# Later row sums, more products held in PSUM, and a depthwise convolution on TensorE alone

## The chip, the cores and the metric

The kernel runs on one core of a Trainium2 chip. The metric is device time in microseconds (us) of one execution.

## The reference

Two blocks follow each other on x of 256 tokens by 1024 channels, in float32. The first has two layers of four attention-like mixers and a gated MLP, the second four layers (retention, conformer convolution, short convolution, retention), each followed by a squared-ReLU MLP. Every stage begins with an RMS norm, which needs the sum of x's squares over the channels for each token. What the change touches, cut from the reference:

```python
def rms_norm(x, g):
    y = xf * lax.rsqrt(jnp.mean(xf * xf, axis=-1, keepdims=True) + RMS_EPS)
    return (y * g.astype(F32)).astype(x.dtype)

def conformer_conv_mixer(x, w_pw1, b_pw1, w_dw, b_dw, ln_g, ln_b, w_pw2, b_pw2):
    h = x @ w_pw1 + b_pw1
    a, gate = jnp.split(h, 2, axis=-1)
    h = a * jax.nn.sigmoid(gate)
    h = causal_depthwise_conv(h, w_dw) + b_dw          # 31 taps for each channel
    mean = jnp.mean(hf, axis=-1, keepdims=True)
    var = jnp.mean(jnp.square(hf - mean), axis=-1, keepdims=True)
    hf = (hf - mean) * lax.rsqrt(var + LN_EPS) * ln_g + ln_b
    h = jax.nn.silu(hf)
    return h @ w_pw2 + b_pw2
```

## The kernel before

x lies with channels on partitions: eight blocks of 128 channels by 256 tokens. A weight matrix product is made in three products of halves (high by high, high by low, low by high), each 128 rows by 128 columns of weights by 256 tokens: `fm_mm` (L294 to L296), and `fm_first` (L325 to L328) for four output blocks at once while x's halves `xh` and `xl` are still being made. `tm_mm` (L301 to L303) has tokens as output rows and 512 weight columns. Weights stream in 636 chunks on SyncE's queue; ScalarE casts the high half (L238), VectorE subtracts for the low half (L239). There are eight PSUM banks.

The norm's factor r is applied behind the first products, so these run on unnormed x. `prep` makes xh and xl of a quarter of x and has ScalarE square it; `stat` is a generator that lets some program steps pass (a step is 12 products), has VectorE add the four quarters of squares (L502, L505), and has TensorE sum them over partitions: `row_sums` (L395) in block 2, `token_sums` (L389) in block 1. `have_r` lets the main program wait, in program order, until r is set. Each stage starts some products before it asks for r and holds their results in PSUM. TensorE executes in program order, so a row sum whose squares are late holds up all products behind it. The order of the program is set by `main` and a `Weave`: at each step of the main generator, every generator in its `light` list advances by one step too.

The conformer's stage takes eight blocks through the gate (`glu`: scale by r, L1429; sigmoid, L1432; product into `cf_p`, padded by 30 tokens, L1435) and then 31 taps. Blocks 0, 1, 6 and 7 are convolved on VectorE (L1374, L1376), block 2 on ScalarE and GpSimd (L1443, L1444), blocks 3 to 5 on TensorE by 31 matmuls each with diagonal 128 by 128 matrices (L1454), which GpSimd builds earlier (L1390). Low halves go to GpSimd in that time (`lo_engine`). Sums for mean and variance come together on VectorE (L1504) and TensorE (L1521, bank `cm`); normalisation and halves `cf_h` and `cf_l` follow block by block, and the last product `cf_w_pw2_2` into the banks `acc`. In the retention, `rotary` (L1309 to L1312) turns q and k on VectorE, then TensorE makes the scores in `bk_ra`, VectorE masks them into `rt_a` (L1266), and TensorE makes the output products `bk_ry` (L1274).

Of the kernel before, what the change touches and what calls it, by code (L numbers as in the profile page):

```python
# [17 lines left out]
P = 128  # L18
# [10 lines left out]
CF_PE = (3, 4, 5)  # L29
CF_DVE = ((0, 1), (6, 7))  # L30
CF_POOL = (2,)
CF_STEP = 4
CF_LATE = 4
CF_GLU = 1
LAG_COLS = (8, 3)
LAG_ROWS = 9
WARM1 = (0, 10, 0, 0)
RET_PRE = 1
# [4 lines left out]
LAG_FINAL = 8  # L43
# [107 lines left out]
for _n, _w in (("norm_mix", 16), ("norm_ffn", 16), ("norm_final", 8), ("norm_g", 128), ("gn_g", 32),  # L151
               ("b_pw1", 16), ("w_dw", 31 * 8), ("b_dw", 8), ("ln_g", 8), ("ln_b", 8), ("b_pw2", 8),
# [39 lines left out]
class Net:  # L192
# [277 lines left out]
    def prep(self, j, gain, final=None):  # L470
# [4 lines left out]
        self.square(j)  # L475
        if j == 3:
            self.r = None
            self.weave.light.append(self.stat(final, False))

    def square(self, j):  # L480

        q = self.g("sq")
        self.sqs = [q] if j == 0 else self.sqs + [q]
        self.nc.scalar.activation(q, self.x[j], AF.Square)

    def add_squares(self, final):
# [14 lines left out]
        for j in range(1, 4):  # L501
            add(q[0], q[0], q[j], op=ALU.add)  # L502
            yield
# [5 lines left out]
    def stat(self, final, root):  # L509
# [101 lines left out]
    def ffn(self, l):  # L611
# [3 lines left out]
        def up(f):  # L615
            sp = [((f * P, P),), ((f * P + P, P),)]
            if f == 0:
                g, u = yield from self.fm_first(l, (("w_gate", sp[0]), ("w_gate", sp[1]), ("w_up", sp[0]), ("w_up", sp[1])))
                ready.append((yield from self.fm_pair("w_gate", l, [((q * P, P),) for q in (2, 3)])))
            else:  # L620
                g = ready.pop() if ready else (yield from self.fm_pair("w_gate", l, sp))
                u = yield from self.fm_pair("w_up", l, sp)
# [510 lines left out]
    def layer1(self, l):  # L1133
# [14 lines left out]
        qb = yield from self.fm_pair("w_in", l, [cols(("a_q", 0, P)), cols(("a_q", P, P))])  # L1148
        y, rb, rb2 = yield from self.have_r()
# [7 lines left out]
        nc.vector.tensor_tensor(zq, qb, rb2, op=ALU.mult)  # L1157
        t1 = yield from self.tm_group("w_in", l, cols("c_i", "c_f", "a_g", "c_v", "a_vs", "a_vw"))
# [7 lines left out]
        zbq = yield from self.fm_scaled(l, [cols(("b_q", 0, P)), cols(("b_q", P, P))], "zbq")  # L1166
# [213 lines left out]
    def diag_taps(self, pool):  # L1380

        self.dg = {}
        for c in CF_PE:
            d = self.t([P, 31, P], "cf_d%d" % c, pool=pool)
            self.dg[c] = d
        for _ in range(12):
            yield
        for c in CF_PE:
            for q in range(31):
                self.nc.gpsimd.tensor_scalar(self.dg[c][:, q, :], self.ident, self.vec("w_dw", q * 8 + c), None, op0=ALU.mult)  # L1390
                if q % 2:
                    yield
# [437 lines left out]
```

## Time and profile before

| | |
|---|---|
| three runs | 2206.72 us median, 2206.69 to 2210.83 |
| profiled execution | 2207.37 us, its span 2205.5 us |
| mean granted TensorE clock | 0.973 of full |
| TensorE busy with matmuls | 2076.8 us, 94% |
| VectorE busy | 1508.8 us, 68% |
| ScalarE busy | 1071.0 us, 49% |
| GpSimd busy | 175.8 us, 8% |

The span is the time from the first to the last recorded instruction, and 1.9 us of the execution's time lie around it. In the rows below, PE is TensorE, PEld its weight loads, DVE VectorE, ACT ScalarE and POOL GpSimd. A float32 matmul leaves two records. In brackets stands how long the engine idled before a record, and for whom.

### The profile page before, as it was taken

The page shows a single profiled execution, that of the slowest core. Times are in us where ns is not written, and L with a number is a line of the kernel's source. Part 1 is how long each engine was busy: PE and PEld are TensorE (multiplying, and loading weights), DVE is VectorE, ACT ScalarE, POOL GpSimd, SP SyncE. Part 2 cuts the span into 40 slices and gives each one's busy share as a digit, 9 for nine tenths or more (in the row PEclk, how much of TensorE's full clock was granted, in tenths as well). Part 3 has the DMA queues.
Part 4 walks back from the last instruction along what each step waited for, and adds up shares of the span by engine and source line. Part 5 has one row for each costly group of instructions (what it writes and reads, how often), then busy time and mean ns, then how long its engine had stood idle before and what let it go on. Part 6 is the DMA issues. An engine that isn't in the chain of part 4 may idle for free.

```text
span 2205.5 us, 40772 instructions
## 1 busy us (share of the span) xinstructions
PE 2076.8 (94%) x16352; PEld 2004.2 (91%) x16352; DVE 1508.8 (68%) x2944; ACT 1071.0 (49%) x2118; POOL 175.8 (8%) x196
## 2 busy tenths in 40 slices
PE   8989999999999899989998689999989999998998
PEld 7879999878999889989997589999989988998998
DVE  6776556677755776675579985558865577667555
ACT  5445445445544444554453364444454454455443
POOL 0000000000000000193007620000000000000000
PEclk9989999999999999999999899999999999999999
DMA  7225554323655533645544035554545554464552
GB/s 272 77 78 172 186 197 154 117 86 108 201 192 182 167 133 136 205 140 192 190 137 142 11 101 185 182 185 144 194 140 192 191 171 136 148 211 145 184 183 82
DMA packets 96174, 344.49 MB, mean 156 GB/s; under 512 B 12016, under 2 KB 12272, under 8 KB 95728
## 3 DMA queue, kind: packets, MB, share of 16 engines
q1 hardware_dynamic: 95840, 341.61, 46.2%
q8 instruction: 128, 2.10, 0.4%
q14 instruction: 62, 0.51, 0.1%
q10 hardware_dynamic: 144, 0.28, 0.0%
HBM read 340.79 MB, written 1.05 MB: 155 GB/s over the span
## 4 chain that ended last, share of the span: by engine, by line
PE 74%; DVE 19%; ACT 4%; issue 2%; DMA 1%; SPq 0%; ACTq 0%; DVEq 0%
PE bk_fm L294 11%; PE bk_fm L295 11%; PE bk_fm L296 11%; PE bk_acc L295 9%; PE bk_acc L296 9%; PE bk_acc L294 9%; DVE lo L239 5%; DVE cf_c L1376 4%; PE bk_tm L301 2%; PE bk_tm L302 2%; PE bk_tm L303 2%; DVE sq L502 1%; PE bk_ss L395 1%; ACT at_s L759 1%; ACT hi L238 1%
## 5 line engine op out<-in xcount | busy, mean ns | idle before, releaser
L239 DVE TENSOR_TENSOR lo<-raw,hi 128x512 fp32r<-128x512 f32 x1240 | 782.9, 688 | 149.2 <-ACT hi L238 148.9
L238 ACT CAST hi<-raw 128x512 fp32r<-128x512 f32 x1272 | 701.5, 619 | 121.5 <-issue 67.0
L294 PE MATMUL bk_fm<-xh,hi 128*128 128x256 f32 x2400 | 690.7, 288 | 0.0
L295 PE MATMUL bk_fm<-xl,hi 128*128 128x256 f32 x2400 | 681.6, 284 | 0.0
L296 PE MATMUL bk_fm<-xh,lo 128*128 128x256 f32 x2400 | 680.5, 284 | 0.0
L294 PE MATMUL bk_acc<-hh,hi 128*128 128x256 f32 x1696 | 473.4, 279 | 0.0
L295 PE MATMUL bk_acc<-hl,hi 128*128 128x256 f32 x1696 | 473.2, 279 | 0.1
L296 PE MATMUL bk_acc<-hh,lo 128*128 128x256 f32 x1696 | 473.0, 279 | 0.0
L294 PEld LDWEIGHTS bk_fm<-xh,hi 128*128 128x128 f32 x2400 | 460.0, 192 | 5.7 <-issue 4.0
L295 PEld LDWEIGHTS bk_fm<-xl,hi 128*128 128x128 f32 x2400 | 459.8, 192 | 1.2
L296 PEld LDWEIGHTS bk_fm<-xh,lo 128*128 128x128 f32 x2400 | 459.7, 192 | 0.0
L295 PEld LDWEIGHTS bk_acc<-hl,hi 128*128 128x128 f32 x1696 | 319.1, 188 | 0.5 <-DVE hl L441 0.5
L296 PEld LDWEIGHTS bk_acc<-hh,lo 128*128 128x128 f32 x1696 | 318.9, 188 | 0.0
L294 PEld LDWEIGHTS bk_acc<-hh,hi 128*128 128x128 f32 x1696 | 318.9, 188 | 0.0
L663 DVE TENSOR_TENSOR ff_t<-ff_t 128x512 f32<-128x512 f32 x64 | 44.5, 695 | 232.5 <-ACT ff_t L662 232.5
L662 ACT ACTIVATE ff_t<-bk_fm 128x512 f32<-128x512 f32 x64 | 38.3, 599 | 250.8 <-PE bk_fm L296 249.7
L440 ACT CAST hh<-ff_t 128x512 fp32r<-128x512 f32 x102 | 63.4, 622 | 124.5 <-DVE ff_t L663 58.4
L441 DVE TENSOR_TENSOR hl<-ff_t,hh 128x512 fp32r<-128x512 f32 x102 | 70.8, 694 | 71.5 <-ACT hh L440 71.5
L1390 POOL TENSOR_SCALAR cf_d<-ident,vecs 128x128 f32<-128x128 f32 x93 | 80.7, 887 | 405.1 <-DVE ff_t L1356 405.1
L325 PE MATMUL bk_fm<-xh,hi 128*128 128x256 f32 x384 | 98.3, 288 | 15.2 <-ACT xh L1673 7.9
L326 PE MATMUL bk_fm<-xh,lo 128*128 128x256 f32 x384 | 97.3, 285 | 0.1
L301 PE MATMUL bk_tm<-hi,xh 128*128 128x512 f32 (+2 forms) x224 | 89.2, 398 | 0.0
(413 smaller groups left out, 2474.4 us busy)
## 6 DMA issues: line engine op xcount, KB each, us to landing
raw<-in_w SPq DMA_DIRECT2D x634, 512.0 KB, 4.4
cw<-in_cw SPq DMA_DIRECT2D x2, 1024.0 KB, 8.4
dt<-in_c SPq DMA_DIRECT2D x2, 768.0 KB, 4.8
x<-in_x SPq DMA_DIRECT2D x4, 256.0 KB, 5.8
raw<-in_w SPq DMA_DIRECT2D x4, 256.0 KB, 5.5
out_y<-x SPq DMA_DIRECT2D x4, 256.0 KB, 2.5
c<-in_c SPq DMA_DIRECT2D x1, 977.0 KB, 10.0
rows<-in_rows SPq DMA_DIRECT2D x1, 456.0 KB, 8.5
```

The lines of the kernel that those rows point to most:

```text
L238: nc.scalar.copy(hi[:, q], raw)
L239: self.lo_engine.tensor_tensor(lo[:, q], raw, hi[:, q].bitcast(F32), op=ALU.subtract)
L294: mm(out, w[0], x[0], start=start, stop=False, skip_group_check=True)
L295: mm(out, w[0], x[1], start=False, stop=False, skip_group_check=True)
L296: mm(out, w[1], x[0], start=False, stop=stop, skip_group_check=True)
L301: mm(out, xh, w[0], start=start, stop=False)
L325: mm(b, w[0], hi, start=k == 0 and i % 2 == 0, stop=False, skip_group_check=True)
L326: mm(b, w[1], hi, start=False, stop=False, skip_group_check=True)
L440: nc.scalar.copy(hi, src)
L441: nc.vector.tensor_tensor(lo, src, hi.bitcast(F32), op=ALU.subtract)
L1376: v.scalar_tensor_tensor(out, src[:, j:j + S], w(j), out, op0=ALU.mult, op1=ALU.add)
L1390: self.nc.gpsimd.tensor_scalar(self.dg[c][:, q, :], self.ident, self.vec("w_dw", q * 8 + c), None, op0=ALU.mult)
```

## The change

Row sums: `stat` takes two numbers, the step at which the adds begin and the step at which the sum is made. In block 1 that is 2 and 9 (adds from 4 and the sum at 8 before), in block 2 6 and 17 (from 5 and at 9), at the final norm 2 and 16. Outside the final norm two of the three adds of quarters are now issued in `prep` already. So that there are products to run until r is there, `ffn` holds a pair of `w_up` blocks too, `layer1` the pair b_q, the retention a second pair (k of head 1), the short convolution two more pairs.

Conformer: all blocks are convolved on TensorE. For each block and each quarter of 32 channels, a transfer on ScalarE's queue makes a copy of 128 partitions, 32 channels by 4 shifts of one token (`cf_x`, four buffers). A matmul with 128 rows and 32 columns (`cf_dg`, built on GpSimd from a table) then does four taps of 32 channels at once. Eight of them cover 32 taps, and four such groups write the four quarters of a bank's partitions: 32 matmuls for each block, 256 in all. The gate's order, the moments and the normalisation stay, with operations of GpSimd moved to VectorE. The last product takes its first five rows for all eight outputs, then the other three output by output.

```diff
-LAG_COLS = (8, 3)
-LAG_ROWS = 9
+LAG_COLS = ((2, 9), 4)
+LAG_ROWS = (6, 17)
-RET_PRE = 1
+RET_PRE = 2
-LAG_FINAL = 8
+LAG_FINAL = (2, 16)
...
         self.square(j)
+        if not final and j > 1:
+            self.add_square(j - 1)
...
-        for _ in range((LAG_FINAL - 6) if final else LAG_ROWS - 4 if root else LAG_COLS[0] - 4):
-            yield
-        yield from self.add_squares(final)
+        add_at, sum_at = LAG_FINAL if final else LAG_ROWS if root else LAG_COLS[0]
+        yield from self.steps(add_at)
+        n = 0
+        for _ in self.add_squares(final):
+            n += 1
+            yield
+        yield from self.steps(sum_at - add_at - n)
...
+        for c in range(NK):
+            w = taps[:, 32 * c:32 * c + 32, None].to_broadcast([P, 32, 32])
+            nc.gpsimd.tensor_tensor(self.dg[:, 32 * c:32 * c + 32, :], eye, w, op=ALU.mult)
...
+            x = self.t([P, 4, CF_U], "cf_x", F32, CF_X, p2)
+            for g in range(4):
+                a = pads[c][32 * g:32 * g + 32, 0:CF_U]
+                src = bass.AP(tensor=a.tensor, offset=a.offset, ap=[a.ap[0], [1, 4], [1, CF_U]])
+                nc.scalar.dma_start(out=x[:, g, :], in_=src)
+            xs[c] = x
+
+        def conv(c):
+
+            yield from self.until(lambda: c in xs)
             b = self.bank("cf")[:, :S]
-            for q in range(31):
-                mm(b, self.dg[c][:, q, :], pads[c][:, q:q + S], start=q == 0, stop=q == 30)
-                if q % 4 == 3:
+            x = xs.pop(c)
+            for m in range(8):
+                for g in range(4):
+                    mm(b[32 * g:32 * g + 32, :], self.dg[:, 32 * c + 8 * g + m, :], x[:, g, 4 * m:4 * m + S], start=m == 0, stop=m == 7)
+                if m % 4 == 3:
                     yield
...
-        for os in ((0, 1, 2, 3), (4, 5), (6,), (7,)):
-            for k in range(NK):
-                for o in os:
-                    b, opens = self.block(acc, o)
-                    self.fm_mm(b, self.take("cf_w_pw2_2", j, k, ((o * P, P),)), hs[k], k == 0 and opens, k == NK - 1)
-                if len(os) > 1 or k % 4 == 3:
+        for k in range(CF_ROWS):
+            for o in range(NK):
+                b, opens = self.block(acc, o)
+                self.fm_mm(b, self.take("cf_w_pw2_2", j, k, ((o * P, P),)), hs[k], k == 0 and opens, False)
+                if o % 4 == 3:
                     yield
+        for o in range(NK):
+            b, _ = self.block(acc, o)
+            for k in range(CF_ROWS, NK):
+                self.fm_mm(b, self.take("cf_w_pw2_2", j, k, ((o * P, P),)), hs[k], False, k == NK - 1)
+            yield
+            f(o)
```

How this moves the instructions is shown at three places. The first is TensorE in the MLP of block 2's first layer, at the row sum (a row is line, operation, what is written and read, and the shape). Before, the sum stands in the middle of the third pair of output blocks:

```order
L294 MATMUL bk_fm_10998<-xh7_89,hi_10850 128x256
L295 MATMUL bk_fm_10998<-xl7_97,hi_10850 128x256
L296 MATMUL bk_fm_10998<-xh7_89,lo_10851 128x256
L395 MATMUL bk_ss_11033<-sq_10823,ones_100 128x256
L294 MATMUL bk_fm_10998<-xh0_82,hi_10885 128x256
L295 MATMUL bk_fm_10998<-xl0_90,hi_10885 128x256
```

Now it stands in the middle of the next pair, behind the rest of the pair above, 48 products of the second weight matrix into `bk_acc` and half of its own pair:

```order
L294 MATMUL bk_fm_11141<-xh7_89,hi_11007 128x256
L295 MATMUL bk_fm_11141<-xl7_97,hi_11007 128x256
L296 MATMUL bk_fm_11141<-xh7_89,lo_11008 128x256
L395 MATMUL bk_ss_11175<-sq_10823,ones_100 128x256
L294 MATMUL bk_fm_11141<-xh0_82,hi_11041 128x256
L295 MATMUL bk_fm_11141<-xl0_90,hi_11041 128x256
```

The sum has moved behind 96 more products of 128x256. The second place is TensorE at the end of the conformer's first projection. Before, two blocks of 31 taps follow the last projection product, then the first mean of two blocks (`bk_cm0`), the third block of taps, and the moments (`bk_cm`):

```order
L296 MATMUL bk_fm_13787<-xh7_89,lo_13671 128x256
L1454 MATMUL bk_cf_13872<-cf_p3_13253,cf_d3_10866 128x256 x31
L1454 MATMUL bk_cf_13986<-cf_p4_13255,cf_d4_10867 128x256 x31
L1491 MATMUL bk_cm0_14089<-cf_c0_13239,mean1_6191 128x256
L1491 MATMUL bk_cm0_14089<-cf_c1_13240,mean1_6191 128x256
L1454 MATMUL bk_cf_14096<-cf_p5_13257,cf_d5_10868 128x256 x31
L1521 MATMUL bk_cm_14180<-cf_sum0_14094,ones_100 128x256
L1521 MATMUL bk_cm_14180<-cf_sum1_14095,ones_100 128x256
L1521 MATMUL bk_cm_14180<-cf_c5_13244,ones_100 128x256
L1521 MATMUL bk_cm_14180<-cf_p5_13257,ones_100 128x256
L1655 MATMUL bk_warm_14185<-hi_13670 128x256 x14
```

Now two blocks of taps stand earlier, between projection pairs, and six follow the last projection product in one go, up to the moments:

```order
L296 MATMUL bk_fm_13770<-xh7_89,lo_13583 128x256
L1447 MATMUL bk_cf_13854<-cf_x_13619,cf_dg_10868 32x256 x32
L1447 MATMUL bk_cf_13889<-cf_x_13624,cf_dg_10868 32x256 x32
L1447 MATMUL bk_cf_13928<-cf_x_13732,cf_dg_10868 32x256 x32
L1447 MATMUL bk_cf_13975<-cf_x_13849,cf_dg_10868 32x256 x32
L1447 MATMUL bk_cf_14019<-cf_x_13967,cf_dg_10868 32x256 x32
L1447 MATMUL bk_cf_14058<-cf_x_14012,cf_dg_10868 32x256 x32
L1513 MATMUL bk_cm_14101<-cf_sum0_13186,ones_100 128x256
L1513 MATMUL bk_cm_14101<-cf_sum1_13187,ones_100 128x256
L1513 MATMUL bk_cm_14101<-cf_c7_13161,ones_100 128x256
L1513 MATMUL bk_cm_14101<-cf_p7_13183,ones_100 128x256
```

The VectorE work that stood between the taps and the moments has no counterpart. The third place is VectorE in the first retention, from k's rotary of head 0 to the mask of its scores. Before, only q of head 1 (`rt_q` from `tr_qc` and `tr_qs`) is turned ahead of the mask (last row):

```order
L1312 TENSOR_TENSOR rt_k_8830<-rt_u_8828,rt_w_8829 128x256
L1340 TENSOR_SCALAR rt_s_8836<-rt_s_8836 128x2
L1342 TENSOR_SCALAR rt_v_8835<-rt_v_8835,rt_s_8836 128x512 x2
L534 SCALAR_TENSOR_TENSOR x0_78<-x0_78,vecs_98,y1_8666 128x256
L1309 TENSOR_TENSOR rt_u_8843<-bk_fm_8746,tr_qc_8813 128x512
L1310 TENSOR_TENSOR rt_w_8844<-bk_fm_8746,tr_qs_8815 128x512
L1311 TENSOR_TENSOR rt_q_8845<-rt_u_8843,rt_w_8844 128x256
L1312 TENSOR_TENSOR rt_q_8845<-rt_u_8843,rt_w_8844 128x256
L239 TENSOR_TENSOR lo_8861<-raw_8654,hi_8860 128x512
L534 SCALAR_TENSOR_TENSOR x0_78<-x0_78,vecs_98,y1_8666 128x256
L1266 TENSOR_TENSOR rt_a_8873<-bk_ra_8868,dt_8495 128x384
```

Now both q and k of head 1 are turned ahead of it:

```order
L1355 TENSOR_SCALAR rt_s_8901<-rt_s_8901 128x2
L1357 TENSOR_SCALAR rt_v_8900<-rt_v_8900,rt_s_8901 128x512 x2
L1324 TENSOR_TENSOR rt_u_8907<-bk_fm_8746,tr_qc_8878 128x512
L1325 TENSOR_TENSOR rt_w_8908<-bk_fm_8746,tr_qs_8880 128x512
L1326 TENSOR_TENSOR rt_q_8909<-rt_u_8907,rt_w_8908 128x256
L1327 TENSOR_TENSOR rt_q_8909<-rt_u_8907,rt_w_8908 128x256
L1324 TENSOR_TENSOR rt_u_8914<-bk_fm_8811,tr_kc_8882 128x512
L1325 TENSOR_TENSOR rt_w_8915<-bk_fm_8811,tr_ks_8884 128x512
L1326 TENSOR_TENSOR rt_k_8916<-rt_u_8914,rt_w_8915 128x256
L1327 TENSOR_TENSOR rt_k_8916<-rt_u_8914,rt_w_8915 128x256
L239 TENSOR_TENSOR lo_8924<-raw_8694,hi_8923 128x512
L1281 TENSOR_TENSOR rt_a_8938<-bk_ra_8933,dt_8495 128x384
```

One rotary of four operations has moved ahead of the mask.

## Rows read from the trace of the kernel before

**Rows 1.** The page's parts 1 and 4: busy time by engine, and the last chain.

```profile
PE 2076.8 (94%) x16352; PEld 2004.2 (91%) x16352; DVE 1508.8 (68%) x2944; ACT 1071.0 (49%) x2118; POOL 175.8 (8%) x196
...
PE 74%; DVE 19%; ACT 4%; issue 2%; DMA 1%; SPq 0%; ACTq 0%; DVEq 0%
```

**Rows 2.** TensorE's waits: us in all, times, longest.

```profile
PE bk_ss L395 <- DVE sq L505: 31.8, 8, 6.8
PE bk_cm L1521 <- DVE cf_sum L1504: 19.4, 1, 19.4
PE bk_ss L389 <- DVE sq L505: 10.3, 4, 4.9
...
PE bk_cf L1454 <- issue: 7.7, 1, 7.7
...
PE bk_acc L295 <- DVE cf_l L1551: 3.8, 4, 1.5
```

**Rows 3.** Row sums on TensorE and VectorE's add before one, in order of time.

```profile
753.21 2.05 PE L395 MATMUL bk_ss<-sq,ones 128*128 128x256 f32 x4 [6.84 <-DVE sq L505]
...
971.61 0.51 DVE L505 TENSOR_TENSOR sq<-sq 128x256 f32<-128x256 f32 x1
...
972.17 1.22 PE L395 MATMUL bk_ss<-sq,ones 128*128 128x256 f32 x2 [6.25 <-DVE sq L505]
...
1163.61 0.70 PE L395 MATMUL bk_ss<-sq,ones 128*128 128x256 f32 x2 [1.73 <-DVE sq L505]
...
1811.54 0.70 PE L395 MATMUL bk_ss<-sq,ones 128*128 128x256 f32 x2 [1.31 <-DVE sq L505]
```

**Rows 4.** Two windows: us, busy (records) of PE, PEld, DVE, ACT, POOL, clock, DMA, GB/s.

```profile
972.83:978.06 5.23, 5.23 (x26) 5.14 (x25) 3.75 (x7) 1.59 (x4) 5.23 (x8) 0.53 0.29 100
...
983.67:989.35 5.68, 5.68 (x51) 5.68 (x49) 2.62 (x5) 1.15 (x2) 5.68 (x8) 1.00 0.89 303
```

**Rows 5.** A window of weight products alone; of the engines PE only.

```profile
1164.00:1194.00 30.00, 30.00 (x254) 1.00 0.41 141
```

**Rows 6.** First retention: a window of one rotary (DVE), and the mask.

```profile
774.27:776.35 2.08, 2.04 (x6) 1.00 0.00 0
...
777.26 0.55 DVE L1266 TENSOR_TENSOR rt_a<-bk_ra,dt 128x384 f32<-128x384 f32 x1
```

**Rows 7.** Windows of the conformer's stage, columns as in the fourth group.

```profile
1147.11:1195.66 48.55, 46.77 (x386) 46.09 (x386) 43.80 (x67) 24.85 (x47) 31.49 (x18) 1.00 0.36 122
...
1203.38:1246.14 42.76, 42.76 (x190) 36.89 (x190) 42.30 (x65) 19.87 (x41) 35.69 (x37) 0.96 0.07 25
...
1265.55:1274.31 8.76, 7.30 (x30) 6.38 (x30) 4.83 (x13) 3.76 (x8) 0.79 (x1) 0.67 0.01 2
...
1274.31:1302.20 27.89, 24.01 (x192) 22.93 (x193) 21.73 (x38) 19.29 (x39) 10.60 (x12) 1.00 0.35 114
```

**Rows 8.** L1454: a window of it alone (PE, PEld); its loads' shortest, median, longest ns.

```profile
1210.00:1240.00 30.00, 29.30 (x137) 25.51 (x136) 1.00 0.05 19
...
L1454 PEld LDWEIGHTS bk_cf<-cf_p,cf_d x186: 187/189/337, 1203.3 to 1245.6; 128*128 128x128 f32 x186
```

**Rows 9.** Tiles of 64 rows: two first records, a window of such tiles (PE).

```profile
142.87 0.39 PE L745 MATMUL bk_s<-dl_k,dl_q 64*128 64x128 f32 x2
...
142.87:144.48 1.61, 1.61 (x17) 1.00 0.01 5
```

**Rows 10.** The conformer's first gate on VectorE.

```profile
1167.72 0.69 DVE L1429 TENSOR_TENSOR ff_t<-bk_fm,rb 128x512 f32<-128x512 f32 x1
1169.27 1.12 DVE L1435 SCALAR_TENSOR_TENSOR cf_p<-ff_t,vecs 128x256 f32<-128x256 f32 x1 [0.85 <-ACT ff_t L1432]
```

**Rows 11.** The page's part 6: a transfer, KB each, us from issue to landing.

```profile
out_y<-x SPq DMA_DIRECT2D x4, 256.0 KB, 2.5
```

More of the change, by code (lines that the diff above doesn't have):

```diff
@@ L500, in add_squares @@
             self.sq2 = t
-        for j in range(1, 4):
-            add(q[0], q[0], q[j], op=ALU.add)
+        for j in range(self.added + 1, 4):
+            self.add_square(j)
             yield
@@ L1399, in conformer @@
         for c in range(NK):
[L1400 removed]
+            a = self.t([P, 32 + S], "cf_p%d" % c, F32, 1, p2)
             nc.gpsimd.memset(a[:, 0:30], 0.0)
+            nc.gpsimd.memset(a[:, 30 + S:], 0.0)
             pads.append(a)
[L1403 to L1425 removed]
+        ready, xs = [], {}
         def glu(c, b, rb2):
@@ L1504, in fold, with after, sp @@
                     e.tensor_tensor(t, a[folded[0]] if len(folded) == 2 else t, a[c], op=ALU.add)
[L1506 to L1516 removed]
+        def after(c, b):
+            nc.scalar.activation(cv[c], b, AF.Identity, bias=self.vec("b_dw", c))
+            yield
+            if c == 1:
+                b = self.bank("cm0")[:, :S]
+                for n in range(2):
+                    mm(b, self.mean1, cv[n], start=n == 0, stop=n == 1)
+                m0.append(self.t([P, S], "cf_m0", F32, 1, p2))
+                nc.scalar.activation(m0[0], b, AF.Identity, scale=NK / 2.0)
+                yield
+            for n in (0, 1) if c == 1 else (c,) if c else ():
+                moments(n, nc.vector)
+                yield
+                fold(n, nc.vector)
+        def sp(b):
+            return ("cf_w_pw1_2", ((b * P, P),))
+        light = self.weave.light
+        begun = 0
+        for c in range(NK + CF_LAG):
+            if c == 0:
+                ready.extend((yield from self.fm_first(j, [sp(0), sp(8), sp(1), sp(9)])))
+            elif 1 < c < NK:
+                ready.append((yield from self.fm_pair("cf_w_pw1_2", j, [sp(c)[1], sp(8 + c)[1]])))
+            if c > 3:
+                _, _, rb2 = yield from self.have_r()
+            if CF_LAG <= c:
+                b = yield from conv(c - CF_LAG)
+                if c - CF_LAG < NK - 1:
+                    light.append(after(c - CF_LAG, b))
+            while c > 3 and ready and begun < CF_X + max(0, c - CF_LAG + 1):
+                light.append(glu(begun, ready.pop(0), rb2))
+                begun += 1
+            if c == NK + CF_LAG - 2:
+                self.want_sqrt()
+        last = NK - 1
+        yield from self.until(lambda: len(folded) == last)
+        nc.scalar.activation(cv[last], b, AF.Identity, bias=self.vec("b_dw", last))
         moments(last, nc.vector)
```

152 lines of the change are left out of this document (43 added, 109 removed).

## The prediction

> **What bounds the kernel now.** I read the page first: TensorE is busy 94% of the span, VectorE 68%, and of the chain that ended last 74% lies on TensorE and 19% on VectorE [rows 1]. So time comes off only where TensorE idles, runs at its lower clock, or does work that goes. The waits of TensorE come next [rows 2]: 31.8 us in eight waits at the row sums (L395) and 10.3 us in four at the column sums (L389), each for the last add of x's squares on VectorE, then 19.4 us for the conformer's moments, 7.7 us before its first tap product and 3.8 us for halves of its last product. Third, one of these places in order of time [rows 3]: the add that ends the sum starts at 971.61 and the sum at 972.17, after 6.25 us of idling; three of the eight are in other kinds of stage (6.84 and 1.31 in the retentions, 1.73 in the conformer). Fourth, what a wait costs beyond itself [rows 4]: after that one, 26 records take 5.23 us at a granted clock of 0.53, the lower level, 1.2 GHz; a little later 51 take 5.68 at 1.00 (2.4 GHz). At the second rate 26 would take 2.90, so the wait costs 2.3 us more. In a long stretch 254 weight products take 30.00 us, 0.118 each [rows 5].
>
> **The sums ahead of the MLPs and the short convolution.** The three other kinds of stage set apart, five waits are left: 31.8 - 6.84 - 1.73 - 1.31 = 21.9 us. The sum moves 96 products back, 96 x 0.118 = 11.3 us; idling began at 972.17 - 6.25 = 965.9, so TensorE comes to it at 977.2. VectorE's own end hardly moves: in its queue two adds come earlier and the last two stand behind the same hidden halves as now with one low half more ahead, so 972.1 becomes about 973. The margin is some 4 us. Held pairs are products that ran anyway. What is late next is r, by 11 us; in an MLP its reader is the stage's end. With 21.9 goes the clock: four of the five waits are long, 4 x 2.3 = 9 at most. I take **-30** (-22 if the clock stays low for other reasons, -31 with all).
>
> **The column sums in block 1.** 10.3 us of waits, and clock: once the 2.3 of above for the longest (4.9), half of it for the two of about 2, together about 3.4. The sum now has 12 products more ahead, and the adds begin two steps earlier. Not all stays: the first layers' chain from r through the scaling to the convolution and rope now has one scaling more ahead of it on VectorE, so I give 5 back for waits behind it: **-8.5** (bounds 0 and -13.7).
>
> **Retention.** The sum goes behind 36 more products of 512 columns and the pair for k of head 1 is held too. Its 6.84 goes. But VectorE does a further rotary before the scores' mask (L1266 at 777.26), whose like for q fills 774.27 to 776.35, 2.1 us [rows 6], and the sum itself comes 1.7 us later than now, since TensorE gets to it only at 746.4 (where the idling before 753.21 began) + 36 x 0.236 = 754.9; 0.236 is an estimate, twice 0.118 for twice the columns. So the first output products come about 3.8 us later than now, with 48 products (5.7) more done by then: **-2** for the first retention, 0 for the second, where 1.31 is all there was. Bounds -6 and +5, the latter if the waits for the mask come twice.
>
> **The conformer.** Its stage is 48.55 + 7.7 + 42.76 + 19.4 + 8.76 + 27.89 = 155.1 us now [rows 7, 2]: products of the first projection, wait, 93 tap matmuls on TensorE, wait for VectorE's taps, moments and normalisation, last product. The taps on VectorE, GpSimd and ScalarE go, and with them the 19.4.
>
> The new tap matmuls are the unknown. There are 256 with 32 output columns and 128 rows, each two records like the 186 of now, which take 29.30 us for 137, 0.214 each [rows 8]. Four of them write the four quarters of the output's partitions. If the four share the array perfectly, 64 groups x 2 x 0.214 = 27.4 us; one after another, 512 x 0.214 = 109.6. No row has tiles that share all rows and split the columns. The nearest have 64 rows each: two of their records start within 0.03 us of each other, and 16, half of 256 columns and half of 128, take 1.61 us (the 17th in the row is a product that ends there) [rows 9], where one after another 8 x 0.214 + 8 x 0.107 = 2.57 is due and in perfect pairs 1.28. That is 1.25 of the perfect time, end of the pipe included, which a long stretch pays less often. Between 27.4 and 27.4 x 1.25 = 34 I take **31**.
>
> The Trainium skill, "TensorE: Matmul & The Clock Gate", Part 3 (Packing small matmuls), gives 2.38 times for three column tiles of 32 and 3.07 for four row tiles; by 2.38 the taps would take 109.6/2.38 = 46 us, an estimate from that page, and the time would be 15 us above mine. No run here shows it yet.
>
> New stage: 384 products of the first projection, 45.4; the sum, 0.4; the wait for the first shifted copies, 3; taps 31; a first mean of four records 0.9; the end of the moments and the normalisation 8.8 as now; the last product 192 x 0.118 = 22.7 with 0.5 of waits, since its first five rows go over all eight outputs and leave each next half eight products' time; at its end 0.5; clock after the waits 2. Together 115.2 of 155.1: **-40** (-44 with perfect tiles, +39 one after another). The 3 us is worked out so: from the sum at 1163.61 [rows 3] to the gate's first step at 1167.72 are 4.1 us, that step starts a chain that ends at 1169.27 + 1.12 [rows 10], 2.7 us, and a transfer of 256 KB lands after 2.5 us [rows 11]; these 9.3 stand against 72 products, 8.5 us. That leaves 0.8, and the copies of four blocks may queue behind each other, so 0 to 8.
>
> At nothing I put GpSimd's eight builds of the new stationaries (the 93 builds of now go, and GpSimd is 8% busy), the 32 small transfers on ScalarE's queue, and the low halves that return from GpSimd to VectorE, which loses its taps. If the builds were late the first tap matmul would wait for them.
>
> **Sum.** -30 - 8.5 - 2 - 40 = -80.5, from the profiled execution's 2207.4 (span 2205.5 and 1.9 around it): 2126.9. The median shown is 0.65 lower, so **2126 us**.
>
> **Rivals.** *Half shared.* If a tile's second record held up the next tile's first, the taps would take 256 x 0.214 = 55 us, 24 more: 2150. For it: a matmul here is two records, and no row splits the columns. Against it: the two records that start together [rows 9] must be of two tiles, since a record of 128 columns lasts 0.107, so a tile's second record did not hold up its neighbour. Chance 0.11.
>
> *The waits come back.* If VectorE, now with earlier adds, is late at the later places too, or the held pairs leave too few PSUM banks, half of the first two terms stays: +19, 2145. Against it: the margin of 4.4 us. Chance 0.07.
>
> *No sharing.* The four column tiles run one after another, and the conformer does not get what it was rebuilt for: 109.6 for the taps, +79, 2205, no change that can be told. Chance 0.03.
>
> *Slower.* One after another, and each record's weight load not hidden either. Loads of this kind last 0.19 us [rows 8]; with a quarter of that exposed on 512 records, 24 us more: 2229. It decides from taps of 31 + 80.5 = 111.5 us on. Against it: loads are busy 2004 us under 2077 us of matmuls [rows 1], all with 128 rows, so they do lie under work on the same rows. Chance 0.05.
>
> The Trainium skill, the same page and part, says that a weight load overlaps running matmuls only where the row group differs; by that rule the slower case would be the likely one. The trace here disagrees for whole-array products; for column tiles no run shows it.
>
> **How the numbers follow.** The sum as worked out has 0.74, with a range of its own of 2106 to 2148. Faster: 0.74 + 0.11 + 0.07 = 0.92; same (within 0.2%, 4.4 us, about what a measurement of this kernel can tell from no change) 0.03; slower 0.05. The range for 8 in 10 takes in the first two rivals, and some of their combination: 2104 to 2166; its low end has perfect tiles, no wait for the copies and the retention's better bound, with little given back in block 1.
>
> **What would show it.** Right: the waits for the last add at the row sums under 5 us in all; a stretch of tap matmuls of about 31 us with groups of four records that start within some 20 ns; no wait for VectorE before the moments; the conformer's stage at about 115 us; the granted clock at 1.00 after the MLPs' sums. Wrong: tap records that start 0.21 apart (no sharing), or pairs (half); waits of 5 us or more for the copies in front of taps; waits in the retention that exceed the 9 us that go.

## The result: 2172.61 us, a gain of less than half the predicted size

| | before | changed |
|---|---|---|
| median (lowest to highest) of four runs | 2208.77 us (2206.69 to 2211.53) | 2172.61 us (2171.1 to 2173.85) |
| ratio of the times, 95% interval | | 0.9835 (0.9818 to 0.9852) |
| profiled execution, its span | 2207.37, 2205.5 us | 2173.64, 2171.6 us |
| mean granted clock | 0.973 | 0.980 |

The changed kernel is faster by 1.65%. The prediction was 2126 us with a range of 2104 to 2166: the sign is right, the size is 46.6 us off, outside the range. The page's parts 1 and 4, answering to [rows 1]:

```profile
PE 2078.1 (96%) x16678; PEld 1997.6 (92%) x16678; DVE 1448.2 (67%) x2863; ACT 1054.9 (49%) x2092; POOL 22.2 (1%) x45
...
PE 82%; DVE 12%; ACT 4%; issue 1%; DMA 0%; ACTq 0%; DVEq 0%
```

TensorE's share of the last chain rises from 74% to 82%, VectorE's falls from 19% to 12%. TensorE's waits are other ones now (us in all, times, longest), beside [rows 2]:

```profile
PE bk_fm L328 <- DVE xl L1670: 8.5, 5, 2.7
PE bk_ry L1289 <- DVE rt_a L1281: 8.1, 4, 3.4
PE bk_acc L295 <- DVE cf_l L1540: 8.1, 5, 4.3
PE bk_s L758 <- DVE df_k L745: 7.6, 2, 3.8
...
PE bk_ra L1277 <- DVE rt_k L1326: 6.2, 2, 4.8
...
PE bk_cf L1447 <- DMA cf_x<-cf_p: 3.8, 2, 3.3
```

The waits for the last add, 31.8 and 10.3 us, are gone from the list, and so are the moments' 19.4. But 8.1 us for the conformer's halves and 7.6 for `df_k` stand there now, and in the retentions 8.1 for the mask (`bk_ry`) and 6.2 for k's rotary (`bk_ra`). To see where the time went, I set the stages side by side. A stage here runs from its first product on x (L325) to that of the next stage, the last one to the start of the last matmul; e4, e6, e12 and e13 are experiments below. One row alone tells 1 or 2 us badly: the mixers of layer 0 took 174.34 to 177.51 us in the changed kernel, e1, e2, e3 and e7, which have them alike.

| stage, us | before | after | e4 | e6 | e12 | e13 |
|---|---|---|---|---|---|---|
| block 1, layer 0: mixers | 171.12 | 175.36 | 172.19 | 173.33 | 175.63 | 167.94 |
| layer 0: MLP | 191.33 | 189.79 | 187.47 | 191.89 | 185.69 | 185.69 |
| layer 1: mixers | 172.13 | 168.24 | 170.93 | 171.48 | 168.85 | 169.67 |
| layer 1: MLP | 190.02 | 189.79 | 187.47 | 193.83 | 185.69 | 185.69 |
| block 2, retention | 219.03 | 218.47 | 220.29 | 220.70 | 217.44 | 217.43 |
| MLP | 196.14 | 202.55 | 187.09 | 197.54 | 196.77 | 185.54 |
| conformer | 161.02 | 133.54 | 162.84 | 162.95 | 133.34 | 124.30 |
| MLP | 193.90 | 188.95 | 186.93 | 195.72 | 185.53 | 185.77 |
| short convolution | 98.53 | 100.15 | 99.38 | 99.33 | 101.30 | 100.06 |
| MLP | 194.95 | 188.94 | 186.93 | 197.00 | 185.77 | 185.77 |
| retention | 208.20 | 212.54 | 212.40 | 208.23 | 211.92 | 207.43 |
| MLP | 193.01 | 187.19 | 185.16 | 194.19 | 183.78 | 183.79 |
| sum | 2189.39 | 2155.51 | 2159.09 | 2206.19 | 2131.71 | 2099.10 |

Against the terms of the prediction, with e4 (the sums without the conformer) as a second measurement:

| term | predicted | after - before | e4 - before |
|---|---|---|---|
| block 2's MLPs and short convolution | -30 | -8.8 | -31.0 |
| block 1 | -8.5 | -1.4 | -6.5 |
| the two retentions | -2 | +3.8 | +5.5 |
| conformer | -40 | -27.5 | +1.8 (old conformer) |
| sum | -80.5 | -33.9 | -30.3 |

Three things stand out. The MLP ahead of the conformer grew by 6.4 us where its like elsewhere shrank by 5 to 6. The conformer gave 27.5 of 40. And all MLPs, in block 1 too, are 2 us slower than in e4, which has the same sums.

**The MLP ahead of the conformer.** In order of time (start, us, engine, line, operation), GpSimd's builds of the new stationaries and VectorE at the head of that stage:

```profile
950.57 17.26 POOL L1406 TENSOR_TENSOR cf_dg<-cf_taps 128x1024 f32<-128x1024 f32 x8 [426.56 <-DMA cf_taps<-in_cft]
...
949.81 0.48 DVE L1670 SCALAR_TENSOR_TENSOR xl<-x,vecs,xh 128x256 fp32r<-128x256 f32 x1
950.21 0.68 DVE L1689 TENSOR_TENSOR x<-x,hg 128x512 f32<-128x512 f32 x1
950.81 2.14 DVE L1670 SCALAR_TENSOR_TENSOR xl<-x,vecs,xh 128x256 fp32r<-128x256 f32 x1
952.87 2.40 DVE L1686 TENSOR_TENSOR hg<-hg,rr_s 128x512 f32<-128x512 f32 x1
955.19 2.12 DVE L1670 SCALAR_TENSOR_TENSOR xl<-x,vecs,xh 128x256 fp32r<-128x256 f32 x1
```

From the moment the first build runs, each VectorE operation on two SBUF operands lasts 2.1 to 2.4 us instead of 0.48 to 0.68. The builds last 17.26 / 8 = 2.16 us each: VectorE gets one operation through per build. The Trainium skill, "SBUF — State Buffer", section "SBUF: two separate sides", says that the two engines share a port pair which one of them holds for a whole instruction when VectorE has two SBUF inputs and GpSimd reads SBUF; the trace agrees, with these numbers. VectorE makes xl there, and TensorE starves (8.5 us at L328). The program spaces the builds six steps apart, but GpSimd had nothing else to do and ran all eight without a gap, once it had its table of taps.

**The conformer's stage**, in windows with the columns of [rows 4], the first five beside [rows 7]: projection up to the wait, the wait for the copies, rest of the projection with the taps and means, moments and normalisation, last product. The sixth is the third again, its tap matmuls alone (PE, PEld), the seventh a stretch of nothing else:

```profile
1151.64:1187.16 35.52, 35.48 (x290) 35.03 (x290) 27.71 (x51) 21.89 (x41) 0.00 (x0) 1.00 0.46 151
1187.16:1190.45 3.29, 0.01 (x1) 0.02 (x1) 1.90 (x5) 0.00 (x0) 0.00 (x0) 0.81 0.82 217
1190.45:1235.70 45.25, 44.68 (x612) 29.42 (x612) 17.18 (x35) 13.89 (x29) 0.00 (x0) 0.94 0.56 157
1235.70:1243.01 7.31, 4.97 (x34) 4.05 (x31) 3.64 (x9) 4.24 (x9) 0.19 (x4) 1.00 0.00 0
1243.01:1280.33 37.32, 28.30 (x192) 27.10 (x193) 22.56 (x49) 20.01 (x40) 0.00 (x0) 0.82 0.27 93
...
1190.45:1235.70 45.25, 32.08 (x512) 17.05 (x512) 0.94 0.56 157
...
1216.00:1234.00 18.00, 18.00 (x340) 10.88 (x336) 1.00 0.50 130
```

The new taps do what they were built for: 512 records are busy 32.08 us, where 31 was predicted, and in the steady stretch 18.00 / 340 = 0.053 us each, a quarter of the 0.214 of a lone one. The weight loads lie under them. The wait for the copies is 3.29 us (3 predicted), moments and normalisation take 7.31 (8.8 predicted). All that is missing stands in one row: the last product, 23.7 us with its waits in the prediction, takes 37.32, at a granted clock of 0.82. In order of time, the first products of it, then VectorE and ScalarE in the loop that feeds it:

```profile
1243.01 0.39 PE L294 MATMUL bk_acc<-cf_h,hi 128*128 128x256 f32 x1 [2.34 <-ACT cf_h L1537]
1247.70 0.58 PE L295 MATMUL bk_acc<-cf_l,hi 128*128 128x256 f32 x1 [4.30 <-DVE cf_l L1540]
...
1246.62 0.69 DVE L239 TENSOR_TENSOR lo<-raw,hi 128x512 fp32r<-128x512 f32 x1 [1.62 <-ACT hi L238]
1247.22 0.42 DVE L1540 TENSOR_TENSOR cf_l<-cf_c,cf_h 128x256 fp32r<-128x256 f32 x1
...
1250.06 0.69 DVE L239 TENSOR_TENSOR lo<-raw,hi 128x512 fp32r<-128x512 f32 x1 [1.62 <-ACT hi L238]
...
1245.03 0.60 ACT L1533 ACTIVATE cf_c<-cf_c,vecs 128x256 f32<-128x256 f32 x1 [1.55 <-DVE cf_c L1532]
1245.66 0.40 ACT L1537 CAST cf_h<-cf_c 128x256 fp32r<-128x256 f32 x1
1245.97 0.61 ACT L238 CAST hi<-raw 128x512 fp32r<-128x512 f32 x1
```

Each block goes from VectorE's scaling to ScalarE's SiLU and two casts, and the low half of the weights (L239) stands on VectorE for the last of these casts, ahead of `cf_l` and of the next block's scaling. The two engines take turns, and a block takes 1250.06 - 1246.62 = 3.44 us. Before, this low half was GpSimd's in that loop (L239 on POOL, shown further down). TensorE waits 4.30 us for `cf_l`, and behind the wait its products start 0.21 us apart, the pace of the lower clock level. Of the 14.6 us over 22.7 the waits for `cf_l` are 8.1, the slower pace of 42 products about 4.0, and the rest lies at the restarts and the end.

### The profile page after: what moved, and what is told of

Read it like the earlier page. It is cut to its first block, busy times and chain, and to the rows that moved or that the text cites. A ratio compares the mean times of both kernels' runs of the same rounds, so it can differ in the third digit from the quotient of the medians.

```text
span 2171.6 us, 41168 instructions
## 1 busy us (share of the span) xinstructions
PE 2078.1 (96%) x16678; PEld 1997.6 (92%) x16678; DVE 1448.2 (67%) x2863; ACT 1054.9 (49%) x2092; POOL 22.2 (1%) x45
## 4 chain that ended last, share of the span: by engine, by line
PE 82%; DVE 12%; ACT 4%; issue 1%; DMA 0%; ACTq 0%; DVEq 0%
PE bk_fm L294 12%; PE bk_fm L296 12%; PE bk_fm L295 12%; PE bk_acc L294 10%; PE bk_acc L296 9%; PE bk_acc L295 9%; DVE lo L239 3%; PE bk_fm L328 2%; PE bk_fm L325 2%; PE bk_fm L326 2%; PE bk_tm L301 2%; PE bk_tm L303 1%; PE bk_tm L302 1%; PE bk_cf L1447 1%; ACT at_s L772 1%
## 5 line engine op out<-in xcount | busy, mean ns | idle before, releaser
L239 DVE TENSOR_TENSOR lo<-raw,hi 128x512 fp32r<-128x512 f32 x1272 | 801.0, 687 | 183.1 <-ACT hi L238 183.0
L294 PEld LDWEIGHTS bk_fm<-xh,hi 128*128 128x128 f32 x2400 | 461.5, 192 | 5.2 <-issue 4.1
L325 PE MATMUL bk_fm<-xh,hi 128*128 128x256 f32 x384 | 100.3, 292 | 14.0 <-ACT hi L238 7.4
L325 PEld LDWEIGHTS bk_fm<-xh,hi 128*128 128x128 f32 x384 | 76.2, 198 | 15.4 <-ACT xh L1666 7.9
```

What stands on the lines that cost most here:

```text
L239: self.lo_engine.tensor_tensor(lo[:, q], raw, hi[:, q].bitcast(F32), op=ALU.subtract)
L294: mm(out, w[0], x[0], start=start, stop=False, skip_group_check=True)
L325: mm(b, w[0], hi, start=k == 0 and i % 2 == 0, stop=False, skip_group_check=True)
```

## The experiments

In what follows a ratio is to runs of the kernel before on the same chip, with its 95% interval. The changed kernel's own is 0.9835.

**e1: the builds on VectorE.** The sixteen operations of half the size are issued four steps apart.

```diff
-        for c in range(NK):
-            w = taps[:, 32 * c:32 * c + 32, None].to_broadcast([P, 32, 32])
-            nc.gpsimd.tensor_tensor(self.dg[:, 32 * c:32 * c + 32, :], eye, w, op=ALU.mult)
-            for _ in range(6):
+        for c in range(2 * NK):
+            w = taps[:, 16 * c:16 * c + 16, None].to_broadcast([P, 16, 32])
+            nc.vector.tensor_tensor(self.dg[:, 16 * c:16 * c + 16, :], eye[:, 0:16, :], w, op=ALU.mult)
+            for _ in range(4):
```

> The table of tap stationaries is built by VectorE in 16 pieces of 128x512, spaced by program steps, in place of GpSimd's 8 of 128x1024. Theory: in the changed kernel GpSimd's eight builds lie at 950.6 to 967.8, and in that time VectorE's operations take 2.1 to 2.4 us in place of 0.5 to 0.7, so the MLP behind the first retention is held up; with the builds gone from GpSimd that stage falls from 202.6 to about 189 us, as the MLP behind the conformer has, and the whole from 2172.6 to about 2159. Rival: the slow stretch comes from the later row sum, or from adds of squares that wait for ScalarE in the preparation; then the stage stays at 200 or more and the whole at 2170 or more.

2161.25 us, 0.9764 (0.9748 to 0.978). The stage falls from 202.55 to 188.93. Some 21 us at its head in windows, changed kernel and then e1, and e1's first build:

```profile
949.09:971.00 21.91, 13.36 (x78) 11.97 (x79) 20.67 (x16) 5.96 (x13) 18.00 (x24) 0.84 0.01 4
```

```profile
950.00:971.00 21.00, 20.02 (x165) 19.73 (x165) 18.34 (x34) 14.57 (x29) 0.00 (x0) 1.00 0.35 115
...
975.26 0.69 DVE L1406 TENSOR_TENSOR cf_dg<-cf_taps 128x512 f32<-128x512 f32 x1
```

TensorE does 165 records instead of 78, VectorE 34 instead of 16. The sixteen builds, 0.68 us each, now come later, from 975.26 on, since they stand in VectorE's own order. So e1 changes the engine and the time at once; e7 keeps both.

**e7: the builds on GpSimd, in 64 pieces.** This asks whether it is GpSimd's work at all or the length of its instructions.

```diff
-            nc.gpsimd.tensor_tensor(self.dg[:, 32 * c:32 * c + 32, :], eye, w, op=ALU.mult)
+            for q in range(8):
+                a = 32 * c + 4 * q
+                w = taps[:, a:a + 4, None].to_broadcast([P, 4, 32])
+                nc.gpsimd.tensor_tensor(self.dg[:, a:a + 4, :], eye[:, 0:4, :], w, op=ALU.mult)
```

> The changed kernel with GpSimd's eight builds of 128x1024 cut into 64 of 128x128, same engine, same place. Theory: a VectorE operation that meets a build waits for the end of that one instruction (2.1 us), so with pieces of about 0.3 us each operation loses 0.3 at most and the MLP behind the first retention falls from 202.6 to about 192 us, the whole to about 2162. Rival: the two engines share their access by time and not by instruction; then the total of GpSimd's time counts, the stage stays at about 202 and the whole at about 2172.

2162.55 us, 0.9797 (0.9774 to 0.982), the stage 190.95. Rows of e7 in order of time:

```profile
950.58 42.91 POOL L1408 TENSOR_TENSOR cf_dg<-cf_taps 128x128 f32<-128x128 f32 x63 [427.02 <-DMA cf_taps<-in_cft]
...
951.30 0.62 DVE L1672 SCALAR_TENSOR_TENSOR xl<-x,vecs,xh 128x256 fp32r<-128x256 f32 x1
951.85 0.88 DVE L1691 TENSOR_TENSOR x<-x,hg 128x512 f32<-128x512 f32 x1
```

VectorE's operations cost 0.62 and 0.88 beside the builds, and now GpSimd pays: 42.91 us for what took 17.26. So with the same engine and the same place, VectorE's wait follows the length of the other engine's instruction, not its work in all. The overlap costs 202.55 - 188.93 = 13.6 us in e1's terms.

**e2: the low half of the weights one block later in the normalisation loop.** The cast stays where it is; its subtraction is kept in a list and issued one block later.

```diff
-                self.split_to(self.cut + 1)
+                for e in rest:
+                    e()
+                rest = []
+                self.split_to(self.cut + 1, rest)
```

> In the conformer's normalisation the low half of a weight piece is put one block later in VectorE's queue than its cast in ScalarE's; nothing else differs. Theory: in the changed kernel the blocks come every 3.45 us because VectorE waits 1.63 us in each for a cast that stands behind this block's own activation on ScalarE; then the blocks come every 2.0 to 2.3 us, the last product's stretch falls from 37.3 to about 25 us, and the whole to about 2160. Rival: the new order of the last product (five rows for all eight outputs) is what costs; then the waits for cf_l stay and the whole is 2170 or more.

2165.19 us, 0.9788 (0.9773 to 0.9802); the conformer's stage falls from 133.54 to 125.48. Rows of e2 in order of time, VectorE and TensorE, then the window of its last product with the columns of [rows 4]:

```profile
1242.87 0.68 DVE L242 TENSOR_TENSOR lo<-raw,hi 128x512 fp32r<-128x512 f32 x1
...
1244.60 0.69 DVE L242 TENSOR_TENSOR lo<-raw,hi 128x512 fp32r<-128x512 f32 x1
...
1240.63 0.38 PE L301 MATMUL bk_acc<-cf_h,hi 128*128 128x256 f32 x1 [2.34 <-ACT cf_h L1544]
1242.21 0.38 PE L302 MATMUL bk_acc<-cf_l,hi 128*128 128x256 f32 x1 [1.20 <-DVE cf_l L1550]
...
1240.63:1268.17 27.54, 24.65 (x193) 24.27 (x193) 21.28 (x47) 19.93 (x40) 0.00 (x0) 0.94 0.39 123
```

A block every 1.73 us, half of 3.44, and 1.20 us of waiting instead of 4.30. The direction is right. The last product falls from 37.32 to 27.54, 9.8 us where 12 were expected; the stage as a whole gives 8.1, since its part ahead of the last product took 1.7 longer in this trace. What is left over 22.7 is 4.8 us: the first wait, 17 products at the pace of the lower clock level (about 1.6) and 1.9 between the last product and the sum behind it.

**e3: one quarter after another.** The loops over quarters and over groups of taps change places: eight matmuls on the same 32 columns follow each other.

```diff
-            for m in range(8):
-                for g in range(4):
+            for g in range(4):
+                for m in range(8):
```

> The 32 tap matmuls of a block are issued quarter by quarter (eight in turn into the same 32 output partitions) in place of one matmul for each quarter in turn. Theory: four neighbours run at once only because they write four different quarters, so the taps take about 110 us in place of 33, and the whole about 2172 + 77 = 2250. Rival: TensorE finds the independent ones further on in its queue, and the time stays within 10 us of 2172.

One run: 2225.79 us, against 2212.11 for the kernel before; the stage takes 188.21, 54.7 more. Its tap matmuls in a window:

```profile
1226.00:1286.00 60.00, 60.00 (x369) 32.28 (x368) 1.00 0.15 39
```

60.00 / 369 = 0.163 us each, three times the changed kernel's and less than a lone one's 0.214. Sharing by four therefore depends on the order in which the quarters are issued. Between runs on different quarters there is still some overlap, which I had not expected.

**e4: the sums alone.** The kernel before with the new lags and held pairs; conformer and its own lag (5, 9) as before, so addresses are as before too.

```diff
+        if root:
+            self.roots = getattr(self, "roots", 0) + 1
+            add_at, sum_at = (5, 9) if self.roots == 2 else LAG_ROWS
```

> The kernel before with the part of the change on row sums, lags and held pairs alone; the conformer's stage keeps its old form and its old lag. Theory, from the stages of the two traces: the MLPs and short convolution give 5 to 8 us each, the first layer and the second retention lose 4 each since all behind r there is one chain; with the old builds the MLP behind the first retention gains too: about -20 in all, 2187. Rival, by the prediction: -40, 2167; or nothing, if held pairs cost banks: 2205.

2180.86 us, 0.9856 (0.9841 to 0.9871). Of the waits for the last add one is left, in the conformer, whose lag is the old one:

```profile
PE bk_ss L395 <- DVE sq L513: 1.7, 1, 1.7
```

The table by terms has what follows: the -30 is confirmed at -31.0 (the four MLPs give 31.9, the short convolution loses 0.9), block 1 gives 6.5 of 8.5, and the retentions lose 5.5. This kernel's MLPs are faster than the changed kernel's by 2 us each. That called for another cause, one that acts on products which the change leaves alone.

**e6: the kernel before, with 32 bytes added to a table.** The change takes 248 columns of tap weights out of `vecs`, which lies ahead of the activations in SBUF: xh, xl and the hidden halves (those of an MLP's hidden values) all move. In e6 only eight unused columns are added.

```diff
-        self.vecs = self.t([P, N_VEC], "vecs", pool=self.cst)
+        self.vecs = self.t([P, N_VEC + 8], "vecs", pool=self.cst)
```

> The kernel before with the same 8 unused columns behind its table of vectors, so that x's halves and all activations lie at multiples of 64 bytes as in the changed kernel; nothing else differs. Theory of the address: a weight product goes from 0.1177 to about 0.1192 us and the time rises by about 20 us, 1% (ratio 1.009). Rival: nothing changes, ratio 1.000.

2223.33 us, 1.0067 (1.0048 to 1.0086): slower, with the same instructions. Windows of weight products alone in block 1, kernel before, e6, changed kernel:

```profile
300.00:340.00 40.00, 40.00 (x343) 40.00 (x342) 21.98 (x35) 18.63 (x34) 0.00 (x0) 1.00 0.49 170
```

```profile
300.00:340.00 40.00, 40.00 (x337) 40.00 (x336) 20.78 (x33) 16.68 (x30) 0.00 (x0) 1.00 0.54 176
```

```profile
300.00:340.00 40.00, 40.00 (x338) 40.00 (x337) 20.64 (x33) 16.80 (x31) 0.00 (x0) 1.00 0.53 178
```

343 records, 337, 338, at a clock of 1.00 each, with no idle time. The move brings the kernel before to the changed one's pace.

**e5: the same eight columns on the changed kernel.**

> The changed kernel with 8 unused columns (32 bytes a partition) behind the table of vectors in SBUF. The change took 248 columns (992 bytes) out of that table, and so moved x's halves and all activations from addresses that are 32 above a multiple of 64 bytes to multiples of 64, as the weights' halves have. In the trace of the changed kernel a weight product takes 0.1192 us where it took 0.1177 before, from the first stage on; in the sums alone, which keep the table, 0.1177. Theory: the address does it, and with the 32 bytes back a product takes 0.1177 in all stages; 14,800 products x 0.0015 = 22 us less, 2151. Rival: the cadence comes from something else in the changed kernel (its 32 transfers on ScalarE's queue, or the chip); then 0.1192 stays and the time is 2172.

2169.22 us, 0.9823 (0.9799 to 0.9847). My first theory, that only the address modulo 64 bytes matters, fell: products from xh and xl came faster, those from the hidden halves slower, and little is left.

**e9: twenty-four columns**, which give xh and xl the remainder by 128 bytes that they had before.

> The changed kernel with 24 unused columns (96 bytes) behind the table of vectors: x's halves then lie 96 and the hidden halves 32 above a multiple of 128 bytes, as in the kernel before. With 8 columns (32 and 96) products from x's halves took 0.1167 to 0.118 us and products from hidden halves 0.119 to 0.121; before they took 0.1184 and 0.1168, in the changed kernel (0 and 64) 0.1199 and 0.1178. Theory: what counts is the remainder by 128 of each moving operand, so both come back to 0.1184 and 0.1168 and the time falls by some 20 us, to about 2153. Rival: the place as a whole counts, or transfers of block 2; then the second block stays near 0.119 and the time near 2165.

2184.59 us, 0.9882 (0.9863 to 0.9901): slower than the changed kernel, so 128 is not it either. I then set the mean distance between starts of successive products (over the whole trace, distances over 0.14 us left out) beside the remainder by 256 bytes of where the moving operand begins; the weights' halves begin at 128.

| remainder | xh, xl | hidden halves |
|---|---|---|
| 32 | | 118.5 to 118.6 ns (e9, e10), 119.4 ns (e11) |
| 96 | 118.3 to 118.4 ns (before, e4) | |
| 128 | 119.9 ns (after, e6) | |
| 160 | 116.8 to 117.2 ns (e5, e11, e12, e13) | 116.7 to 116.9 ns (before, e4, e12, e13) |
| 192 | | 117.8 ns (after, e6) |
| 224 | 120.0 ns (e9, e10) | 119.9 ns (e5) |

The changed kernel and e6 have the same remainders at addresses 1024 bytes apart, and the same pace. But the hidden halves lie at the same address in e10 and e11 and differ by 0.9 ns, so the remainder of the moving operand is not the whole of it.

**e12: the changed kernel with both at 160**, nothing else changed: eight columns behind the table, and an unused tile of 48 columns behind x's halves.

```diff
+        self.t([P, 48], "gap", pool=self.act)
```

> The changed kernel, of which nothing is altered but where the activations lie in SBUF: 8 unused columns behind the table of vectors and 48 behind x's halves, so that x's halves and the hidden halves both lie 160 above a multiple of 256 bytes (the weights' halves lie 128 above). So far products from x's halves took, by remainder of 256: 96 0.1184, 128 0.1199, 160 0.1167, 224 0.1200; from hidden halves 32 0.1186 to 0.1195, 160 0.1168, 192 0.1178, 224 0.1190 to 0.1200. Theory: the remainder by 256 sets it, so both take 0.1167 to 0.1169 and the time is some 7400 x 0.0032 + 5088 x 0.001 = 29 us under the changed kernel, about 2144 (ratio 0.971). Rival: the two settle each other, or it is no matter of a remainder; then hidden halves take 0.118 or more and the ratio is 0.977 or more.

2148.39 us, 0.9714 (0.9697 to 0.9732), 24 us under the changed kernel's median; by the two ratios, each to its own runs of the kernel before, it is 27. The window of above:

```profile
300.00:340.00 40.00, 40.00 (x345) 40.00 (x344) 23.08 (x37) 19.35 (x35) 0.00 (x0) 1.00 0.51 165
```

**e8: the factor earlier in the chains.** In block 1's mixers the sum at step 8, its spreading one step earlier and no held pair of b_q; in the second retention the lags (5, 9) and one held pair.

```diff
-            for _ in range(LAG_COLS[1]):
+            for _ in range(3 if self.first else LAG_COLS[1]):
...
-                for a in (S, D + S)[:RET_PRE]:
+                for a in (S, D + S)[:2 if j == 0 else 1]:
```

> The changed kernel with the row sums of the attention-like layers at the place they had (step 8, no extra pair held) and the second retention's sum at its old step with one pair held; the earlier adds stay. Theory: in these stages all behind the factor r is one chain, so a later sum delays the stage: the first layer falls from 175.4 to about 172, the second retention from 212.5 to about 209, and the second layer stays at 168 to 169, since its adds come early now; about -7 in all, 2165. Rival: the layers lose for their held pairs' banks or not at all, and the waits for the squares come back: 2172 or more.

2163.5 us, 0.9797 (0.9777 to 0.9817). Layer 0's mixers fall from 175.36 to 167.68, layer 1's rise from 168.24 to 170.14, the second retention returns to 208.25. In order of time, the first scaling by r in layer 0 and the scores' wait there, kernel before and then the changed one, and the scaling in e8:

```profile
29.47 0.69 DVE L1153 TENSOR_TENSOR zkv<-bk_fm,rb 128x512 f32<-128x512 f32 x1 [0.55 <-ACT rb L548]
...
111.75 0.50 PE L745 MATMUL bk_s<-df_k,df_q 32*128 32x128 f32 x4 [0.16 <-DVE df_k L732]
```

```profile
33.02 0.69 DVE L1167 TENSOR_TENSOR zkv<-bk_fm,rb 128x512 f32<-128x512 f32 x1
...
115.56 0.80 PE L758 MATMUL bk_s<-df_k,df_q 32*128 32x128 f32 x4 [3.79 <-DVE df_k L745]
```

```profile
28.41 0.69 DVE L1175 TENSOR_TENSOR zkv<-bk_fm,rb 128x512 f32<-128x512 f32 x1 [0.59 <-ACT rb L569]
```

**e10: e1, e2, e8's edits for layer 0 and the second retention, and e9's columns together.**

> The changed kernel with all that the runs pointed to: the stationaries built by VectorE, low halves one block later in the normalisation, the first layer's sum at its old step without a held pair, the second retention's sum at its old step with one pair, and the 24 columns. Theory, if the parts add: -14, -8, -7, -4 and -20 from 2172: about 2120. Rival: the parts hide each other; 2135 or more.

2151.64 us, 0.9741 (0.9725 to 0.9757). 33 us under e9, as the parts apart would have it: 13.6 + 8.1 + 7.7 + 4.3 = 33.7. The gain expected from the address did not come, since e9's did not.

**e11: the same with both operands at other remainders**, eight columns and an unused tile of 16 columns behind x's halves: x's at 160, hidden halves at 32.

> The same as the mended kernel, but with x's halves and the hidden halves both 32 above a multiple of 128 bytes (8 columns behind the table, 16 behind the activations of x). Theory of the remainder: both kinds of product at their best, 0.1167 and 0.1168, some 7200 products x 0.0015 = 11 us under the mended kernel, about 2109. Rival: within 3 us of the mended kernel.

2134.11 us, 0.9663 (0.9643 to 0.9683): xh and xl gained (116.8 ns), the hidden halves did not (119.4).

**e13: the same edits and both at 160.**

> The mended kernel with x's halves and the hidden halves both at 160. Theory: against the run with both at 32 of 128 (x's halves at 160, hidden halves at 32 of 256; 2134) the hidden products fall from 0.1194 to 0.1168, 5088 x 0.0026 = 13 us: 2121, ratio 0.960. Rival: no gain, ratio 0.966.

2117.36 us (2116.9 to 2118.47), 0.9577 (0.9562 to 0.9592). It beats both kernels, by 55 us the changed one.

## Why the prediction was wrong, and where it was right

**Right: the term of -30.** e4 gives -31.0. That the margin of 4 us at the sums would hold is confirmed; the rival of returning waits did not occur there. Of the edits it is the later sum with its held pairs that does this: the adds issued early stand in `prep`, which the stages of this term do not pass through. In the MLP behind the conformer the last add starts 20.12 us behind the first product in e4, against 19.51 before, and the sum at 25.90.

**Right: the taps.** 31 us predicted, 32.08 measured. The rivals of half sharing, no sharing and of exposed weight loads are refuted by 0.053 us for a record; e3 shows what a poor order would have cost. The Trainium skill, "TensorE: Matmul & The Clock Gate", Part 3, has 2.38 times for three column tiles; here four give 0.214 / 0.053 = 4.0, and the measurement decides.

**Failed: "At nothing I put GpSimd's eight builds of the new stationaries".** I argued with GpSimd's 8% load and asked only whether the builds would be late. They were in time; they stopped VectorE. 13.6 us (e1), with the mechanism shown from the other side by e7. The 93 builds of the kernel before gave little warning: beside them, at 951.76, xl took 0.59 us instead of 0.48. But rows of its normalisation loop, where GpSimd makes the low halves of weights, were there to read:

```profile
1276.41 1.48 DVE L1551 TENSOR_TENSOR cf_l<-cf_c,cf_h 128x256 fp32r<-128x256 f32 x1
...
1280.85 0.43 DVE L1551 TENSOR_TENSOR cf_l<-cf_c,cf_h 128x256 fp32r<-128x256 f32 x1
...
1274.86 2.76 POOL L239 TENSOR_TENSOR lo<-raw,hi 128x512 fp32r<-128x512 f32 x2 [2.49 <-ACT hi L238]
```

Beside GpSimd's subtraction (1.29 to 1.35 us each) VectorE's `cf_l` took 1.48 us, and without it 0.43.

**Failed: "the last product 192 x 0.118 = 22.7 with 0.5 of waits".** It took 37.3. I put the low halves' return to VectorE at nothing by VectorE's total load. In this loop the load does not matter: the low half waits for a ScalarE cast behind the SiLU, and the scaling of the next block stands behind it. e2 gives 9.8 of the 13.6 back in the last product itself. The other 3.8 are, by e2's rows, the first wait, the lower clock level behind it and the end, for which the stage's sum had too little.

**Failed: the chains in block 1 and the retentions, "0 for the second".** By its sum the term of block 1 was nearly right: 6.5 of 8.5 in e4, where the addresses are the old ones. What failed in it is layer 0. r is used 3.5 us later in layer 0: the scaling of `zkv` starts at 33.02 instead of 29.47. I had given 5 us for it in the block; layer 0 alone lost 4.2 and gained 7.7 when mended (e8). The first retention gained 0.6 where 2 was due. The second lost 4.3: it got the later factor and the second held pair in full, with 1.31 us of waiting to win. That these edits are the cause in the second e8 shows, though not which of its edits does how much. The step that failed is the waits behind the factor, which were priced as a shift of 3.8 us under 5.7 us of products. The kernel before had these:

```profile
PE bk_ry L1274 <- issue: 2.2, 1, 2.2
PE bk_ry L1274 <- DVE rt_a L1266: 2.1, 2, 1.4
...
PE bk_ra L1262 <- DVE rt_k L1311: 0.2, 1, 0.2
```

That is 4.5 us, against 8.1 + 6.2 = 14.3 now: 9.8 came, more than the 6.84 + 1.31 that went.

**Not in the prediction: the address.** The diff's smaller table moves each activation by 992 bytes, and I priced the table at nothing without naming it. On the kernel before, a move to the changed kernel's remainders costs 16.8 us between the traces (e6). On the changed kernel the old remainders were not tried; e12 shows that better ones give it 24.

These causes sum to 13.6 + 8.1 + 7.7 + 4.3 + 16.8 = 50.5 us, against a miss of 46.6. They were measured apart and partly on different kernels, and layer 0's 7.7 is more than the 4.2 that it lost, so the agreement is within several us and in part luck. e13, which keeps the change and mends all of these points, is at 2117, 9 us under the forecast, but with products faster than those of the kernel before, which the forecast did not have.

## What to carry to other kernels

Work that is hidden by an idle engine still has to be asked which ports and queues it shares: read how long the neighbour's operations last beside it, and place it beside operations that it does not stop. In a loop that goes to and fro between two engines, one operation more that waits for the other engine sets the period, whatever the engines' loads. When a change resizes any buffer, compare the pace of an untouched stretch first; here a record count in a 40 us window told in one line that something other than the edit had moved.

## What the runs showed of the hardware

The pace of back-to-back products depends on where the moving operand begins in SBUF: 116.7 ns at remainder 160 by 256 bytes to about 120 at 128 or 224, with weights at 128, worth 24 us here from two unused pieces of SBUF (e12). What in the chip causes it, why e10 and e11 differ at one address, and whether it is the difference to the weights' address that counts, no run here tells apart: the weights were never moved.

Beside a GpSimd instruction on two SBUF operands, a VectorE operation on two SBUF operands lasted about as long as that instruction: 2.1 to 2.4 us beside builds of 2.16, 1.48 beside low halves of 1.29 to 1.35, where 0.43 to 0.68 is usual.

Four column tiles of 32 that follow each other in turn shared the array in full (0.053 against 0.214 us), and eight in a row on the same tile did not (0.163).
